# A two-path decoder step on one core: the conv's shifted input copied on chip, the sample issued 15 units later, its decode held back beside attention, and one norm's waits filled

## The chip, the cores and the metric

The program runs on one core of one Trainium2 chip. A core has five engines with queues of their own: TensorE (PE in the profile, PEld for its weight loads), VectorE (DVE), ScalarE (ACT), GpSimd (POOL) and SyncE (SP, which here only issues DMAs). ScalarE and GpSimd issue DMAs too. The metric is the device time of one execution in microseconds; smaller is better.

## What is computed

The reference runs one trunk over two inputs: a prompt (512 tokens, no past) and a sample (8 sequences of 4 new tokens, each with 2048 past keys and values in pages). Width 1024, 16 heads of 64, two layers. Layer 0 is a convolution module and an MLP; then keys and values are projected; layer 1 is attention and an MLP.

```python
def post_norm_residual(x, y, gate, g, b):
    return layer_norm(DEEPNORM_ALPHA * x + (1.0 + gate) * y, g, b)

def conformer_conv(h, conv_prev, ...):
    a, g = jnp.split(h @ pw1_w + pw1_b, 2, axis=-1)
    u = a * jax.nn.sigmoid(g)
    full = jnp.concatenate([conv_prev, u], axis=1)
    y = depthwise_conv(full, dw_w, width=31) + dw_b
    y = jax.nn.silu(layer_norm(y, ln_g, ln_b))
    return y @ pw2_w, full[:, -30:]

def stick_breaking(q, k, v, bias, q_pos, k_pos):
    z = q . k * HEAD_DIM ** -0.5 + bias
    log_rem = where(mask, log_sigmoid(-z), 0)
    after = suffix sum of log_rem over the later keys
    w = where(mask, exp(log_sigmoid(z) + after), 0)
    return w . v
```

Every sub-layer takes h = x * (1 + scale) + shift with scale, shift and gate from a product of silu(c) with ada_w. The MLP is square(relu(h @ w1)) @ w2 with 4096 inner columns. Outputs are y, the new conv state and the new keys and values of both inputs.

## The kernel before

**Layout.** The prompt stands feature by feature: 8 tiles of 128 features x 512 tokens. Its weights come in by ScalarE's DMA queue (stage), are split on ScalarE (whi) and VectorE (wlo) into a high and a low part, and every product is three matmuls (lines 327, 330, 331; tiles pw in the conv's first product, pd elsewhere). The sample has 32 rows only. Its products take the weights as the moving operand straight from a load on SP's queue (sw, tiles w_acc and sd_acc), and its norms are small steps on VectorE with a sum over features by two tiny matmuls (smp).

**Order of the work.** Sample and prompt are two generators, `sample()` and `prompt()`, and a loop at the end of the kernel advances the one whose clock is behind. Each yield adds a cost: DEC_COST 10 for a step of the sample's decode, ML_COST 2.6 for a piece of the prompt's MLP, AT_COST 12 for one of eight head pairs of the prompt's attention. The sample's clock starts at CLK0 = -20, that is 20 units ahead. The order that comes out is static: each engine has one queue, worked in order. A scheduler may still move an instruction by its priority.

**The conv.** The prompt's gated product u of the 8 feature tiles (k) goes two ways. For two of them (TAPS) VectorE does the 31 taps itself (line 690, tile v out of upad). For the other six u is stored to DRAM (ud, line 877, GpSimd's queue) and read back four times, shifted by 0 to 3 columns (ur, line 703, GpSimd's queue, two buffers): 32 channels times 4 shifts fill the 128 partitions, and 64 products of 128 x 32 weights (wk, made on VectorE, line 707) give one cv tile (line 713). Its statistics (lnT transposes on TensorE, bn on VectorE) follow for each tile, then the norm: VectorE makes mean and rstd, a diagonal matrix dg, and a product with ones spreads them over the partitions (mb, rb, line 386); lines 420 and 421 apply them.

**The other norms** of the prompt work alike; make_h (lines 441 to 466) then gives the split operands xhi (ScalarE) and xlo (VectorE) for the next product. ada_B (line 246) are products of the modulation with weights loaded on SP's queue (adaw), issued between.

**The decode.** For each of 8 sequences s there are 4 key steps, a weights step and 4 value steps. A key step gathers kraw by an indirect DMA of GpSimd (index tile krow), transposes it on VectorE in 128 x 512 pieces (kt, line 1065) and multiplies with qb (zt, line 1071). The weights step has two scans (fx, line 1089), the product z_s (line 1103) and transposes wT. A value step gathers vt (index tile vrow) and multiplies (av, line 1122). krow and vrow come from the page table by 16 small operations of VectorE and two more (lines 1036 to 1040).

**The prompt's attention** works head pair by head pair on units of query blocks: logits pz, two sigmoids on ScalarE (afx, as), a scan on VectorE (line 1423), a product (line 1424), transposes awt, products with the values oP, and at the end of a pair xlo (line 1440).

**The end.** The last MLP block runs in two halves of 256 tokens (v, line 1469), with transposes lnT back to token rows (yt), statistics bn, and for each half mean and rstd by small steps (lines 431 to 438). Of the first half two yt tiles go over ScalarE and GpSimd (lines 1482 to 1484, with nmr = -mean x rstd from VectorE), the other six over VectorE (lines 1486 and 1488). The sample's result is yrow (lines 1167 and 1168), stored on SP's queue as the yt tiles are.

## Time and profile before

| | us |
|---|---|
| median of 3 runs | 1649.97 (1649.86 to 1650.26) |
| the profiled execution's own time | 1648.19 |
| its span, first to last instruction | 1646.4 |
| TensorE busy | 1554.2 (94%) |
| VectorE busy | 955.3 (58%) |
| ScalarE busy | 569.1 (35%) |
| GpSimd busy | 171.8 (10%) |
| mean DMA rate | 249 GB/s |

Busy times are sums over the whole span, in which stages with different limits follow one another: conv product (to about 160 us), conv and its norm (to 270), MLP 0 (330 to 797), keys, values and q (to 990), attention (to 1115), output product and norm (to 1225), MLP 1 (to 1632) and the last norm. So they are read again by stretch. A matmul's end is modelled, and a busy TensorE need not run at its peak: the granted clock (1.00 is 2.4 GHz, 0.50 is 1.2 GHz) stands beside each stretch.

### The profile page before, as it was taken

The page shows a single profiled execution, that of the slowest core. Times are in us where ns is not written, and L with a number is a line of the kernel's source. Part 1 is how long each engine was busy: PE and PEld are TensorE (multiplying, and loading weights), DVE is VectorE, ACT ScalarE, POOL GpSimd, SP SyncE. Part 2 cuts the span into 40 slices and gives each one's busy share as a digit, 9 for nine tenths or more (in the row PEclk, how much of TensorE's full clock was granted, in tenths as well). Part 3 has the DMA queues.
Part 4 walks back from the last instruction along what each step waited for, and adds up shares of the span by engine and source line. Part 5 has one row for each costly group of instructions (what it writes and reads, how often), then busy time and mean ns, then how long its engine had stood idle before and what let it go on. Part 6 is the DMA issues. An engine that isn't in the chain of part 4 may idle for free.

```text
span 1646.4 us, 25072 instructions
## 1 busy us (share of the span) xinstructions
PE 1554.2 (94%) x10297; PEld 1078.2 (65%) x10297; DVE 955.3 (58%) x1822; ACT 569.1 (35%) x905; POOL 171.8 (10%) x197
## 2 busy tenths in 40 slices
PE   6999989989999999999899899889899999999996
PEld 4666325656777777777477675557767767656886
DVE  4599536475676655665644448985765434332547
ACT  2322114262332333323332545852362323223332
POOL 1110200000112121110012012021002100000001
PEclk9999999999999999999999999999999999999998
DMA  9898879688667767676888878365546585995221
GB/s 321 267 338 298 241 271 368 240 327 313 230 230 278 281 248 251 215 258 230 323 286 297 330 255 325 109 238 193 202 154 232 181 332 181 353 345 190 83 74 52
DMA packets 148261, 409.23 MB, mean 249 GB/s; under 512 B 8197, under 2 KB 74021, under 8 KB 123555
## 3 DMA queue, kind: packets, MB, share of 16 engines
q1 hardware_dynamic: 48771, 161.86, 26.3%
q0 software_dynamic: 22944, 149.07, 25.2%
q10 hardware_dynamic: 76432, 96.70, 17.6%
q8 instruction: 81, 1.33, 0.3%
q14 instruction: 33, 0.27, 0.0%
HBM read 390.56 MB, written 17.88 MB: 248 GB/s over the span
## 4 chain that ended last, share of the span: by engine, by line
PE 75%; issue 9%; DMA 7%; DVE 6%; ACT 2%; POOL 1%; DVEq 0%; POOLq 0%; ACTq 0%; SPq 0%
PE pd L327 18%; PE pd L331 17%; PE pd L330 17%; PE zt L1071 3%; PE sd_acc L551 3%; PE av L1122 3%; PE cv L713 2%; DMA adaw<-in_ada_w_dram 2%; PE w_acc L578 2%; PE pw L327 1%; PE pw L330 1%; PE pw L331 1%; DMA stage<-in_conv_pw_w_dram 1%; PE ada_A L246 1%; PE lnT L366 1%
## 5 line engine op out<-in xcount | busy, mean ns | idle before, releaser
L319 DVE TENSOR_TENSOR wlo<-stage,whi 128x1024 fp32r<-128x1024 f32 x184 | 223.7, 1218 | 219.9 <-ACT whi L316 219.6
L316 ACT CAST whi<-stage 128x1024 fp32r<-128x1024 f32 x184 | 191.6, 1046 | 415.2 <-PE pd L331 355.4
L327 PE MATMUL pd<-xhi,whi 128*128 128x512 f32 (+1 forms) x832 | 320.5, 387 | 6.0 <-ACT xhi L454 2.7
L331 PE MATMUL pd<-xlo,whi 128*128 128x512 f32 (+1 forms) x832 | 312.7, 385 | 9.2 <-DVE xlo L460 9.0
L330 PE MATMUL pd<-xhi,wlo 128*128 128x512 f32 (+1 forms) x832 | 318.8, 384 | 2.3 <-DVE wlo L319 2.2
L1065 DVE STREAM_TRANSPOSE kt<-kraw 128x512 f32<-128x512 f32 x256 | 164.3, 686 | 124.0 <-DMA kraw<-in_cache_k_dram,krow 77.5
L327 PE MATMUL pd<-h2h,whi 128*128 128x512 f32 (+1 forms) x544 | 206.5, 388 | 1.6 <-DVE v L1240 1.0
L330 PE MATMUL pd<-h2h,wlo 128*128 128x512 f32 (+1 forms) x544 | 205.1, 382 | 0.0
L331 PE MATMUL pd<-h2l,whi 128*128 128x512 f32 (+1 forms) x544 | 205.0, 383 | 0.0
L331 PEld LDWEIGHTS pd<-xlo,whi 128*128 128x128 f32 x832 | 156.5, 192 | 64.7 <-issue 18.0
L327 PEld LDWEIGHTS pd<-xhi,whi 128*128 128x128 f32 x832 | 160.4, 193 | 56.3 <-issue 13.5
L330 PEld LDWEIGHTS pd<-xhi,wlo 128*128 128x128 f32 x832 | 160.6, 193 | 41.7 <-issue 11.0
L1240 DVE SCALAR_TENSOR_TENSOR v<-pd,mod_B,v 128x512 f32<-128x512 f32 x120 | 87.8, 745 | 117.7 <-PE pd L331 117.4
L1043 POOL DMA_INDIRECT kraw<-in_cache_k_dram,krow x64 | 65.4, 1022 | 625.4 <-DVE kt L1065 391.4
L327 PEld LDWEIGHTS pd<-h2h,whi 128*128 128x128 f32 x544 | 101.9, 188 | 34.9 <-issue 10.4
L1215 ACT ACTIVATE relu<-pd 128x512 f32<-128x512 f32 (+1 forms) x68 | 38.9, 572 | 239.1 <-PE pd L331 233.9
L331 PEld LDWEIGHTS pd<-h2l,whi 128*128 128x128 f32 x544 | 101.8, 188 | 28.6 <-issue 9.4
L330 PEld LDWEIGHTS pd<-h2h,wlo 128*128 128x128 f32 x544 | 102.2, 188 | 25.0 <-issue 6.7
L1043 POOL DMA_INDIRECT vt<-in_cache_v_dram,vrow x64 | 67.0, 1047 | 270.1 <-PE av L1122 220.2
L1071 PE MATMUL zt<-kt,qb 128*32 128x128 f32 x2048 | 75.5, 279 | 5.6 <-DVE kt L1065 5.6
L1071 PEld LDWEIGHTS zt<-kt,qb 128*32 128x32 f32 x2048 | 52.7, 110 | 30.9 <-issue 17.5
L368 DVE BATCH_NORM_STATS2 bn<-lnT 128x6 f32<-128x128 f32 x160 | 36.6, 287 | 61.4 <-PE lnT L366 61.1
(300 smaller groups left out, 1928.1 us busy)
## 6 DMA issues: line engine op xcount, KB each, us to landing
sw<-in_mlp_w_dram SPq DMA_DIRECT2D x64, 1024.0 KB
stage<-in_mlp_w_dram ACTq DMA_DIRECT2D x64, 1024.0 KB
adaw<-in_ada_w_dram SPq DMA_DIRECT2D x40, 1024.0 KB
stage<-in_conv_pw_w_dram ACTq DMA_DIRECT2D x10, 1024.0 KB
adaw<-in_ada_w_dram SPq DMA_DIRECT2D x16, 512.0 KB
swkv<-in_w_kv_dram SPq DMA_DIRECT2D x8, 1024.0 KB
stage<-in_w_kv_dram ACTq DMA_DIRECT2D x8, 1024.0 KB
ur<-ud POOLq DMA_DIRECT2D x24, 270.0 KB, 6.6
```

Source lines behind the costliest of these rows:

```text
L316: ins = nc.scalar.copy(hi, st[:, :, c0 : c0 + cw])
L319: ins = vec.tensor_tensor(lo, st[:, :, c0 : c0 + cw], hi.bitcast(F32), op=ALU.subtract)
L327: first = mm(out, whi, xh, start=start, stop=False)
L330: mm(out, wlo, xh, start=False, stop=False)
L331: latest[:] = [mm(out, whi, xl, start=False, stop=stop)]
L551: mm(acc[32 * g : 32 * g + 32, :], hT[:, kk * 2 + kp, :], blk[:, kp * D + c * 512 : kp * D + c * 512 + 512], start=(kk == 0), stop=(kk == ...
L1043: nc.gpsimd.indirect_dma_start(out=out, out_offset=None, in_=cache.rearrange("g (r e) h d -> (g r) (e h d)", e=2), in_offset=bass.Indirect ...
L1065: ins = vec.transpose(kt[:, 2 * x : 2 * x + 2, :], raw[x].rearrange("p (e c) -> p e c", e=2)[:, :, c0 : c0 + 256])
L1071: behind(mm(zt[u][32 * g : 32 * g + 32, f * P : f * P + P], qb[:, u, hh * 8 + bl].rearrange("p x q -> p (x q)"), kt[:, :, bl * 32 : bl * 3 ...
L1122: behind(mm(av[32 * g : 32 * g + 32, :], wT[u][:, i, e, a, :], vt[:, e * D + u * 512 : e * D + u * 512 + 512], start=(a == 0 and i == 0), ...
L1215: latest_act[:] = [act(r, a, AF.Relu)]
L1240: ins = vec.scalar_tensor_tensor(v[kt][:, ts], a, gt[:, kt, 8:9], v[kt][:, ts], op0=ALU.mult, op1=ALU.add)
```

## The change

Seven things are changed. (1) CLK0 goes from -20 to -5. (2) AT_COST goes from 12 to 4. (3) For the six conv tiles ud, its padding and the ur loads are gone: u is written into the tile y, and 16 copies of 32 partitions x about 512 columns, with two memsets, build ur. For the first two tiles all copies are ScalarE's, spread over the first product; for the other four half are VectorE's. (4) krow and vrow are made where the sample's first dense product is issued (the column of row numbers comes with c1), and bias_p and the page table load behind the axd store. (5) The sample's state_out (the urow copies and eight stores) stands ahead of its MLP 0 instead of behind. (6) One norm (after MLP 0) has 4 + 5 + 4 idle products of 128 x 128: behind the last lnT, behind mb, and ahead of the next pd. (7) nmr has the norms' priority.

```diff
-CLK0 = -20.0
+CLK0 = -5.0
...
-AT_COST = 12.0
+AT_COST = 4.0
...
+                idle_products(mb, self.fill[0], self.last)
                 self.spread(mv[:, b0:b1, 0], mb)
+                idle_products(rb, self.fill[1], last_spread[0])
                 self.spread(rstd_of(mv[:, b0:b1, 1], b1 - b0), rb)
+                waiting[:] = [(self.fill[2], last_spread[0])]
                 return mb, rb
+    waiting = []
+
+    def idle_products(out, n, after):
+        for _ in range(n):
+            after = order(mm(out[:, 0:P], onesm, onesm, start=True, stop=True), after)
...
-    def conv_load(k):
+    def conv_load(k, both):
         raw[k] = pld.tile([P, 4, T + 28], F32, tag="ur", bufs=2, name="ur")
-        for j in range(4):
-            pdma(raw[k][32 * j : 32 * j + 32], ud[k].rearrange("(g c) t -> c g t", g=4)[:, :, j : j + T + 28])
+
+        vec.memset(raw[k][:, :, 0 : CW - 1], 0.0)
+        vec.memset(raw[k][:, :, T + CW - 4 :], 0.0)
+        for g in range(4):
+            for j in range(4):
+                out = raw[k][32 * j : 32 * j + 32, g, CW - 1 - j : min(T + CW - 1 - j, T + 28)]
+                src = y[k][32 * g : 32 * g + 32, 0 : out.shape[-1]]
+                if both and (g + j) % 2:
+                    vec.tensor_copy(out, src)
+                else:
+                    order(nc.scalar.copy(out, src), last_whi[0])
+                    yield
...
-                u = tmp("u")
+                u = y[kt]
             vec.scalar_tensor_tensor(u, acc[0], pcol(R_PWB, kt), sg, op0=ALU.add, op1=ALU.mult)
-            if kt not in TAPS:
-                u_dma = pdma(ud[kt][:, CW - 1 : T + CW - 1], u)
...
             if kt in REST[:2]:
-                conv_load(kt)
+                loads.append(conv_load(kt, False))
+            for _ in itertools.islice(itertools.chain(*loads), 5 if kt < KT - 1 else 32):
+                pass
             some_taps(5)
...
         s_ln(n)
+        state_out()
         n = yield from s_mlp(n, 0)
-        state_out()
...
-        nrm = Norm()
+        nrm = Norm(fill=(4, 5, 4))
         yield from p_mlp(*hl, v, 0, nrm, H_0A, H_0B)
...
-                    vec.scalar_tensor_tensor(nmr, mean, -1.0, rstd, op0=ALU.mult, op1=ALU.mult)
+                    with tc.high_priority(LN_PRI):
+                        vec.scalar_tensor_tensor(nmr, mean, -1.0, rstd, op0=ALU.mult, op1=ALU.mult)
```

The static order of the two kernels shows what the two planner numbers move. Line numbers in the changed kernel are larger by 3 to 21 (1065 is 1083, 1423 is 1443, 1424 is 1444, 1440 is 1460, 1469 is 1489, 1486 to 1488 are 1507 to 1509).

VectorE amid the prompt's attention, before (afx, as: one head pair's scans and products; kt: the decode's transposes):

```order
L1065 STREAM_TRANSPOSE kt<-kraw 128x512 x2
L1423 SCALAR_TENSOR_TENSOR afx<-afx 128x384 x2
L1424 TENSOR_TENSOR as<-as,afx 128x383
L1440 TENSOR_TENSOR xlo<-oP,xhi 128x512
L1424 TENSOR_TENSOR as<-as,afx 128x383
L1065 STREAM_TRANSPOSE kt<-kraw 128x512 x2
L1423 SCALAR_TENSOR_TENSOR afx<-afx 128x512 x2
L1065 STREAM_TRANSPOSE kt<-kraw 128x512 x2
L1424 TENSOR_TENSOR as<-as,afx 128x511 x2
L1423 SCALAR_TENSOR_TENSOR afx<-afx 128x128
```

Six kt transposes of the decode stand among ten operations of the attention here. The same head pair's place in the changed kernel:

```order
L1444 TENSOR_TENSOR as<-as,afx 128x127
L1444 TENSOR_TENSOR as<-as,afx 128x255
L1444 TENSOR_TENSOR as<-as,afx 128x127
L1444 TENSOR_TENSOR as<-as,afx 128x255
L1443 SCALAR_TENSOR_TENSOR afx<-afx 128x384 x2
L1444 TENSOR_TENSOR as<-as,afx 128x383
L1460 TENSOR_TENSOR xlo<-oP,xhi 128x512
L1444 TENSOR_TENSOR as<-as,afx 128x383
L1443 SCALAR_TENSOR_TENSOR afx<-afx 128x512 x2
L1444 TENSOR_TENSOR as<-as,afx 128x511 x2
```

The six transposes are gone from this place. Over the whole attention kt falls from 42 to 18; on TensorE the rows of zt there fall from 176 to 96 and those of av from 40 to 16. The removed steps come behind the attention, and the sample's products with wo, which stood at the 3428th of the prompt's 4416 full-width products, now stand at the 3780th; its w1 blocks go from the 3585th to the 3952nd and its w2 blocks from the 3753rd to the 4135th, ending at the 4298th.

VectorE in the norm ahead of MLP 0's first product, before (v, xlo: the prompt's norm and operands; krow, sv, sred: the sample's index arithmetic and norm):

```order
L420 TENSOR_TENSOR v<-v,mrb 128x256
L1040 TENSOR_SCALAR krow<-krow,c_3339 128x64
L1040 TENSOR_SCALAR vrow<-vrow,c_3339 128x64
L539 TENSOR_TENSOR sv<-sv,sax 128x256
L421 TENSOR_TENSOR v<-v,mrb 128x256
L460 TENSOR_TENSOR xlo<-h,xhi 128x256
L420 TENSOR_TENSOR v<-v,mrb 128x256
L513 TENSOR_REDUCE sred<-sv 128x32
L421 TENSOR_TENSOR v<-v,mrb 128x256
L460 TENSOR_TENSOR xlo<-h,xhi 128x256 x3
```

Four of these rows are the sample's. The same steps of the prompt in the changed kernel:

```order
L473 TENSOR_TENSOR xlo<-h,xhi 128x256
L433 TENSOR_TENSOR v<-v,mrb 128x256
L434 TENSOR_TENSOR v<-v,mrb 128x256
L473 TENSOR_TENSOR xlo<-h,xhi 128x256
L433 TENSOR_TENSOR v<-v,mrb 128x256
L434 TENSOR_TENSOR v<-v,mrb 128x256
L473 TENSOR_TENSOR xlo<-h,xhi 128x256
L433 TENSOR_TENSOR v<-v,mrb 128x256
L434 TENSOR_TENSOR v<-v,mrb 128x256
L473 TENSOR_TENSOR xlo<-h,xhi 128x256
```

The sample's index arithmetic and norm are gone from between them; the norm now stands behind, at the prompt's next v (row 459 on), and the index arithmetic near the span's beginning.

VectorE at the end, behind the prompt's last v (bn: statistics, the second half's; yt: the prompt's result), before:

```order
L1469 SCALAR_TENSOR_TENSOR v<-pd,mod_B_6802,v 128x256 x2
L368 BN_STATS bn_13510<-lnT 128x6 x6
L376 BN_AGGR mv<-bn_13510 128x2 x2
L1486 SCALAR_TENSOR_TENSOR yt<-yt,mv,gb 128x512
L431 TENSOR_SCALAR ve<-mv 128x2
L1486 SCALAR_TENSOR_TENSOR yt<-yt,mv,gb 128x512 x3
L432 TENSOR_SCALAR rw<-ve 128x2
L434 TENSOR_SCALAR vh<-ve 128x2
```

The first half's small steps and nmr are through by then. In the changed kernel, with the first half's small steps and nmr among them:

```order
L1489 SCALAR_TENSOR_TENSOR v<-pd,mod_B_6981,v 128x256
L371 BN_STATS bn_13590<-lnT 128x6 x6
L445 TENSOR_SCALAR rw<-ve 128x2
L447 TENSOR_SCALAR vh<-ve 128x2
L371 BN_STATS bn_13590<-lnT 128x6 x2
L446 TENSOR_SCALAR rs<-rw 128x2
L371 BN_STATS bn_13590<-lnT 128x6 x4
L449 TENSOR_TENSOR rw<-rs 128x2
L379 BN_AGGR mv<-bn_13590 128x2 x2
L450 TENSOR_TENSOR rw<-rw,vh 128x2
L1507 SCALAR_TENSOR_TENSOR yt<-yt,mv,gb 128x512
```

The first half's rstd (rw, rs on 128 x 2) is still being made between the second half's statistics. VectorE some twenty rows later:

```order
L451 SCALAR_TENSOR_TENSOR rs<-rw,rs 128x2
L450 TENSOR_TENSOR rw<-rw,vh 128x2
L1498 SCALAR_TENSOR_TENSOR nmr<-mv,rs 128x2
L1509 SCALAR_TENSOR_TENSOR yt<-yt,rs,gb 128x512 x2
L451 SCALAR_TENSOR_TENSOR rs<-rw,rs 128x2
```

Before the change nmr stood ahead of all of these; now it stands behind 12 statistics and four yt steps. On TensorE the sample's yrow products stood at the 4057th of the prompt's 4416 full-width products and now stand at the 4388th, among the last lnT.

## Rows read from the trace of the kernel before

**Rows 1.** The page's busy times: engine, us, share of the span, instructions.

```profile
PE 1554.2 (94%) x10297; PEld 1078.2 (65%) x10297; DVE 955.3 (58%) x1822; ACT 569.1 (35%) x905; POOL 171.8 (10%) x197
```

**Rows 2.** Busy by stretch: length, PE, PEld, DVE, ACT, POOL, clock, DMA share, GB/s.

```profile
200.00:275.00 75.00, 65.18 (x432) 27.13 (x432) 41.19 (x106) 24.27 (x38) 5.45 (x10) 0.91 0.84 303
300.00:350.00 50.00, 43.05 (x291) 29.13 (x289) 34.85 (x136) 17.78 (x35) 0.00 (x0) 0.94 0.61 223
1000.00:1050.00 50.00, 43.71 (x450) 25.66 (x450) 46.79 (x84) 32.34 (x64) 8.76 (x8) 0.93 0.68 258
1050.00:1115.00 65.00, 55.78 (x630) 35.91 (x627) 58.22 (x103) 43.12 (x85) 9.91 (x10) 0.97 0.53 183
1350.00:1510.00 160.00, 159.62 (x811) 99.81 (x811) 54.74 (x77) 43.83 (x61) 0.00 (x0) 1.00 0.77 286
1625.00:1646.00 21.00, 7.02 (x57) 6.38 (x55) 17.15 (x55) 4.40 (x17) 5.50 (x4) 0.71 0.26 100
```

**Rows 3.** TensorE's waits over the span: us in total, times, longest.

```profile
PE pd L331 <- DVE xlo L460: 9.0, 6, 2.9
...
PE zt L1071 <- DVE kt L1065: 5.6, 3, 2.2
```

**Rows 4.** TensorE in order of time, in the conv: start, us.

```profile
208.71 6.14 PE L713 MATMUL cv<-ur,wk 128*32 128x512 f32 x32 [4.30 <-DMA ur<-ud]
```

**Rows 5.** TensorE's groups, 160 to 233 us: busy, mean ns, idle before.

```profile
L713 PE MATMUL cv<-ur,wk 128*32 128x512 f32 x384 | 50.0, 624 | 4.3 <-DMA ur<-ud 4.3
```

**Rows 6.** Three tiles' instructions: duration ns min/median/max, first and last start.

```profile
L946 DVE COPY qr<-qr x3: 684/684/687, 394.0 to 395.4; 32x1024 f32<-32x1024 f32 x3
...
L1261 DVE COPY ucrow<-ucT x2: 668/670/671, 245.5 to 246.1; 30x512 f32<-30x512 f32 x2
...
L556 ACT COPY sd_sb<-sd_acc x5: 562/586/589, 189.9 to 1509.3; 128x512 f32<-128x512 f32 x5
```

**Rows 7.** VectorE's groups, 160 to 233 us.

```profile
L368 DVE BATCH_NORM_STATS2 bn<-lnT 128x6 f32<-128x128 f32 x24 | 5.4, 286 | 20.3 <-PE lnT L366 20.3
L707 DVE TENSOR_TENSOR wk<-c,wtap 128x1024 f32<-128x1024 f32 x4 | 4.9, 1225 | 3.8 <-PE cv L713 3.8
...
L690 DVE SCALAR_TENSOR_TENSOR v<-upad,prm,v 128x512 f32<-128x512 f32 x3 | 2.3, 777 | 0.0
```

**Rows 8.** VectorE's groups, 328 to 348 us.

```profile
L1037 DVE TENSOR_SCALAR vrow<-ptab 32x32 int32<-32x32 int32 x8 | 1.4, 174 | 0.0
```

**Rows 9.** A stretch of the norm after MLP 0, columns as in Rows 2.

```profile
816.00:819.00 3.00, 3.00 (x12) 1.10 (x12) 2.93 (x6) 3.00 (x5) 0.00 (x0) 0.50 1.01 408
```

**Rows 10.** VectorE's groups in the attention, 1000 to 1112 us.

```profile
L1065 DVE STREAM_TRANSPOSE kt<-kraw 128x512 f32<-128x512 f32 x38 | 24.7, 686 | 5.5 <-DMA kraw<-in_cache_k_dram,krow 5.5
...
L1089 DVE TENSOR_TENSOR_SCAN fx<-fx 128x512 f32<-128x512 f32 x2 | 2.4, 1220 | 0.0
```

**Rows 11.** TensorE's groups in the attention, 1000 to 1115 us.

```profile
L1071 PE MATMUL zt<-kt,qb 128*32 128x128 f32 x320 | 15.1, 292 | 5.6 <-DVE kt L1065 5.6
...
L1122 PE MATMUL av<-vt,wT 128*32 128x512 f32 x64 | 9.7, 599 | 1.1 <-DMA vt<-in_cache_v_dram,vrow 1.1
```

**Rows 12.** The sample's last w2 block and its last store, in order of time.

```profile
1508.12 1.06 PE L551 MATMUL sd_acc<-sw,h2T 128*32 128x512 f32 x8
...
1544.33 0.35 SPq L1169 DMA_DIRECT2D out_dram<-yrow  x1
```

**Rows 13.** VectorE and GpSimd at the end, in order of time.

```profile
1629.66 2.44 DVE L1488 SCALAR_TENSOR_TENSOR yt<-yt,rs,gb 128x512 f32<-128x512 f32 x2
1632.02 0.86 DVE L1469 SCALAR_TENSOR_TENSOR v<-pd,mod_B,v 128x256 f32<-128x256 f32 x2
...
1640.35 2.74 DVE L1488 SCALAR_TENSOR_TENSOR yt<-yt,rs,gb 128x512 f32<-128x512 f32 x4
...
1630.17 3.06 POOL L1483 TENSOR_TENSOR yt<-yt,gb 128x512 f32<-128x512 f32 x2 [310.90 <-ACT yt L1482]
1633.18 2.48 POOL L1484 TENSOR_TENSOR yt<-yt,gb 128x512 f32<-128x512 f32 x2
```

More of the change, by code (lines that the diff above doesn't have):

```diff
@@ L67 @@
 NR = 56
[L69 removed]
+C1_W = 128 + 32 + 64 + 32 + 3
 C2_W = 512 + 512 + 128 + 128 + 20
@@ L679, in yoco_step_kernel @@
     raw = {}
+    loads = []
     TAPS = (0, 2)
@@ L717, in conv @@
         if k in REST[:-2]:
-            conv_load(REST[REST.index(k) + 2])
+            for _ in conv_load(REST[REST.index(k) + 2], True):
+                pass
     sy = sfm("sy", "sv", 2)
@@ L1176, in p_tiles @@
         out = [pm("pd")[:, 0 : ts.stop - ts.start] for _ in w]
+        while waiting:
+            idle_products(out[0], *waiting.pop())
         for k in range(nk):
```

42 lines of the change are left out of this document (19 added, 23 removed).

## The prediction

> **What bounds the kernel now.** I read the whole-span busy table first, then busy time by stretch, then who TensorE waited for, then the groups of instructions inside the two stretches the change reorders, and last the end in order of time. TensorE is busy 1554.2 us of the 1646.4 us span [rows 1], so a change that leaves TensorE's work as it is can only win what stands between its work: idle time and time at a lower granted clock. The stretches show where that is [rows 2]. From 1350 to 1510 us, where the sample's MLP runs beside the prompt's, TensorE is busy 159.62 of 160 us: no room. In the attention, 1000 to 1115 us, it is busy 43.71 + 55.78 = 99.5 of 115 us, at 0.93 and 0.97 of full clock, while VectorE is busy 46.79 + 58.22 = 105.0. VectorE sets the pace there. From 300 to 350 us (the norm ahead of MLP 0's first product) 6.95 us are idle and the clock takes some 43.05 x 0.06 = 2.6 us more. From 1625 to the end only 7.02 of 21 us are TensorE's; the rest is VectorE's last norm. The list of waits names the same engine: it stood 9.0 us for xlo and 5.6 for kt, both VectorE's [rows 3].
>
> The profiled execution took 1648.19 us, 1.79 us outside its span, and the median of three runs is 1649.97. I make the sum on the profiled execution and add 1.8 us for the median.
>
> **Conv input copied on chip.** Gone are 24 loads of ur, 6 stores of ud and the padding stores, all on GpSimd's queue, and the one wait that they caused: TensorE stood 4.30 us for ur, and the 32 products behind it took 6.14 us [rows 4], where the other eleven groups of 32 took (50.0 - 6.14) / 11 = 4.0 [rows 5]. So 4.3 + 2.1 = 6.4 us can go. In its place each of six blocks needs 16 copies of 32 x 512, eight of them on VectorE and eight on ScalarE (the first two blocks all on ScalarE). The trace has no such copy. The nearest rows: VectorE copied 32 x 1024 from SBUF to SBUF in 684 ns, half of which with a share of fixed cost is about 0.37 us; from PSUM it copied 30 x 512 in 670 ns; ScalarE took 586 ns for 128 x 512 from PSUM [rows 6]. I take 0.37 on VectorE, the same kind of source and target, and keep 0.67 as the upper end. Per block VectorE then has 8 x 0.37 = 3.0 us of copies, one wk (1.23), eight statistics (8 x 0.23 = 1.8) and 14/6 filter taps of 0.78 (1.8), which the change puts later [rows 7]: 7.8 us, 8.6 with the two memsets and small sample steps. TensorE's 64 products and their transposes take 8.0 + 0.6 us. They are level, so some of the wait comes back: 2 to 4 us in all. ScalarE's eight copies, 8 x 0.59 = 4.7 us, lie inside the block. So the conv itself gives -3. The sample 15 units later leaves the conv's norm fewer filler blocks, and puts sample norm steps and two urow copies ahead of its second spread: +3, since that stretch (200 to 275 us) is already idle 9.8 us [rows 2]. Together 0, from -4 to +6; at 0.67 us a copy 4 x 8 x 0.3 = +10.
>
> The Trainium skill (VectorE: DVE Perf Modes, section "Mode 2×_2P — use both read ports for one tensor") says that a one-source fp32 copy runs at twice the rate only with source and target in SBUF and an outermost dimension that is even, or odd and equal on both sides. The two copy rows agree with the SBUF half of it (684 ns for 1024, 670 ns for 512 from PSUM); that copies of 511 elements keep the rate no run here shows.
>
> **Index arithmetic moved.** krow and vrow leave the norm of MLP 0 and run about 80 us into the span, where VectorE already works hard on the first product's operands. With what goes with it, +1 us (0 to +4).
>
> **MLP 0's first norm.** Sixteen small operations with 1.4 us on vrow alone [rows 8], as much on krow, and the sample's post-norm chain (about 10 us of VectorE in all between 328 and 348 us) no longer stand among the make_h steps that xlo waits for. There are 6.95 + 2.6 = 9.5 us to be had [rows 2]. I take 7, because the prompt's own chain of some 24 half-tile operations stays: -7 (-11 to -2).
>
> **Fills at one norm.** At the norm after MLP 0 the granted clock reads 0.50, the lower of TensorE's two levels, from 816 to 819 us, though TensorE is busy all of it [rows 9]: 3 x 0.5 = 1.5 us lost there, perhaps 3 with its neighbours. Thirteen 128 x 128 products fill idle time and can keep the clock. But ada_B blocks that wait for weights now stand between them ahead of mb and rb, and so do the sample's wT transposes: 0 (-3 to +4).
>
> **Attention.** A unit of prompt attention now counts 4 instead of 12, so eight units advance the clock by 32 instead of 96, and the planner issues less decode work among them. On VectorE 42 kt transposes among the attention become 18; two scans fx, two qb, two z_s, am and the small steps leave too. 24 x 0.686 = 16.5 us, and fx 2.4 [rows 10], and about 4.4 for the rest: 23 us off the engine that sets the pace. TensorE loses zt 176 to 96 rows of the order, 45% of 15.1 us, and av 40 to 16, 60% of 9.7 [rows 11]: 6.8 + 5.8 = 12.6 us. That work isn't gone: it lands in MLP 1, where TensorE has no room, and lengthens it by its full size. Net 23 - 12.6 = about -10 us. If VectorE also keeps the 5.5 us that it stood for kraw [rows 10], -14 at best; if the attention turns TensorE-bound (99.5 - 4.7 for the clock - 12.6 = 82 us of work against VectorE's 82, so they are level) and keeps its present share of idle time, 13%, the stretch shrinks by 20 and the net is -7; -4 is my upper end. What is late next in the attention is TensorE itself.
>
> **The end.** The sample's last store was issued at 1544.33 [rows 12], 100 us ahead of the end; now yrow is issued 28 full-width products (6.5 us) ahead of TensorE's last, and its store directly ahead of the prompt's last stores on SP's queue. On VectorE the sample's last norm (some 25 operations) stands among the prompt's last v, and the first half's statistics come after yrow. nmr, which ran before 1629.66, now comes behind the second half's statistics: after the last v remain 12 statistics instead of 6, four yt steps and some 20 small ones, about 9.3 us, then nmr. From nmr on, ScalarE's yt (0.8) and GpSimd's 3.06 + 2.48 us [rows 13] make 6.9 us with the gaps. Before, from the last v (1632.02 + 0.86) to the last yt's end (1640.35 + 2.74) were 10.2 us; now 9.3 + 6.9 = 16.2: +6. With a little standing of TensorE for smp and yrow +7 (+3 to +11).
>
> VectorE's two yt steps beside GpSimd took 2.44 us, 1.22 each, while four of them later took 2.74, 0.69 each [rows 13]. They slow one another, and my 6.9 us holds that: six at up to 1.22 are 7.3. The Trainium skill (SBUF — State Buffer, section "Who interferes with whom") states it harder: an operation of VectorE with two inputs in SBUF and one of GpSimd that reads SBUF exclude one another; an estimate by that is 6 x 0.69 + 5.54 = 9.7 us in place of 6.9, and the end +10. It speaks against this change; the row of 1.22 us shows a part of it.
>
> **Sum.** Conv 0, index arithmetic +1, MLP 0's norm -7, fills 0, attention -10, the end +7: -9 us. 1648.2 - 9 = 1639 profiled, 1641 us as a median, -0.55%.
>
> **Rivals.** (A) Work is only moved. If TensorE bounds the attention as soon as VectorE is relieved, or MLP 1 gets new waits for the decode's operands, the attention gives 0: 1 - 7 + 7 = +1, so 1650 us (no change). For it speaks that the two engines come out level, and that kt and kraw now arrive in MLP 1; against it that VectorE was busy over 90% of the attention and TensorE 86%. Chance 0.14. (B) The sample becomes the end. Its last chain of product, reduce, mean, reduce, small steps and transposes had 35 us from the end of the last w2 block (1508.12 + 1.06) to its store (1544.33) [rows 12]; now about 90 full-width products of 0.23 us and some small ones lie between, about 23 us. TensorE's queue is in order, so smp or yrow that waits stops the prompt's products behind it. From the point where the chain needs over 23 us each us more is an us of time; at 32 us it is +9 on top of the +7, and with -5 from the attention and -2 from MLP 0's norm instead of my values, 1650 + 1 + 16 - 7 = 1660 us (slower). The chain's own durations add up to about 11 us, which speaks against; its 35 us before speak for. Chance 0.13. (C) VectorE binds the conv: the copies cost 0.67 us, the conv +10: 1651 us, no change. Chance 0.08. (D) Better than forecast: the conv's 6.4 us go entirely, the clock holds at the filled norm, the attention -14: 1641 - 3 - 3 - 4 = 1631. Chance 0.15. The forecast has 0.50.
>
> **Chances and range.** A measurement of this kernel tells about 0.2%, 3.3 us, from no change. The forecast with its own range 1633 to 1646 and (D) are faster, with a little of (A) and (C): 0.68. Within 0.2%: most of (A) and (C), 0.16. Slower: (B) and the tails of (A) and (C), 0.16. The range for 8 in 10 goes from 1626 to 1654.
>
> **What would show it.** Attention: VectorE's busy time near 82 us there and TensorE's idle time below 10; if the stretch is 20 us shorter and MLP 1 12 us longer, the step is right. MLP 0: the wait for xlo around 330 us gone. Conv: copy rows near 0.37 us, no wait for ur over 2 us a block. Filled norm: a granted clock of 1.00 through the stretch and no wait for adaw over 2 us. The end: some 27 us without much of TensorE instead of 21, GpSimd's yt last. The forecast is wrong if smp or yrow shows waits of several us, or if the first stretch after attention has new idle time.

## The result and the profile of the changed kernel

The changed kernel takes 1668.33 us (median of four runs, 1666.27 to 1669.43) against 1650.12 for the kernel before on the same chip: 1.0119 [1.0103, 1.0136], 1.2% slower. The forecast was 1641 and the range ended at 1654. The profiled execution took 1668.12 us, 1.8 outside its span, as before.

The busy page of the changed kernel, engines in the order of [rows 1]:

```profile
span 1666.3 us, 25161 instructions
PE 1559.4 (94%) x10323; PEld 1084.3 (65%) x10323; DVE 973.3 (58%) x1866; ACT 607.8 (36%) x969; POOL 153.0 (9%) x164
```

The span grew by 19.9 us, TensorE's busy time by only 5.2. To see where, I cut both spans at the same counts of the prompt's full-width products and took, of each piece, the idle time of TensorE plus its busy time times (1 - granted clock). I call that the loss of a piece:

| piece (products) | loss before | loss after | forecast of the difference |
|---|---|---|---|
| 0 to 500: first product, conv, its norm | 40.1 | 37.9 | 0, index arithmetic +1 |
| 500 to 700: start of MLP 0 | 10.8 | 6.5 | -7 |
| 2000 to 2300: the filled norm | 9.3 | 9.5 | 0 |
| 2500 to 2630: ahead of the attention | 7.5 | 10.2 | none |
| 2690 to 2850: the attention and part of the output product | 23.1 | 36.6 | -10 |
| 2850 to TensorE's last product | 17.0 | 17.1 | none |
| behind it | 13.1 | 19.2 | +7 |
| all, with small pieces | 121.0 | 137.2 | -9 |

The other 3.7 us of the 19.9 are TensorE's own work at full clock; the fills, whose 26 instructions take some 3 us, count as work here. The windows of the changed kernel that answer to [rows 2] (busy us of each engine, granted clock, DMA share, GB/s); the last is the stretch behind TensorE's last product:

```profile
200.00:275.00 75.00, 67.56 (x422) 33.91 (x415) 52.40 (x138) 30.51 (x48) 3.83 (x7) 0.93 0.59 220
300.00:350.00 50.00, 45.09 (x314) 29.57 (x311) 30.44 (x99) 29.91 (x57) 0.00 (x0) 0.97 0.90 325
1000.00:1050.00 50.00, 39.92 (x387) 24.80 (x388) 38.95 (x66) 25.50 (x50) 6.22 (x6) 0.81 0.56 205
1050.00:1115.00 65.00, 52.52 (x463) 35.31 (x462) 48.22 (x82) 45.98 (x91) 0.00 (x0) 1.00 0.15 41
1646.90:1666.30 19.40, 0.45 (x2) 0.05 (x1) 14.63 (x42) 2.96 (x10) 5.12 (x4) 0.50 0.29 108
```

From 1000 to 1050 us VectorE is busy 38.95 us where it was busy 46.79 [rows 2]: the relief came. TensorE stands 10 us all the same, and its clock is 0.81. The list of what TensorE waited for (us in all, times, longest) has a new first line, a wait inside the prompt's own attention that was 2.3 us before, and a second one for whi (ScalarE's split of the weights), 2.5 us before, of which 6.7 us come in one piece ahead of the attention; xlo and kt are a little smaller than in [rows 3], and ur is gone from it:

```profile
PE oP L1455 <- ACT aw L1449: 20.2, 20, 3.0
PE pd L330 <- ACT whi L318: 9.1, 5, 6.7
...
PE pd L334 <- DVE xlo L473: 7.8, 9, 1.8
PE zt L1089 <- DVE kt L1083: 4.9, 4, 3.1
```

### The profile page after: what moved, and what is told of

It is laid out like the page before. It is cut to its first block, busy times and chain, and to the rows that moved or that the text cites. A ratio compares the mean times of both kernels' runs of the same rounds, so it can differ in the third digit from the quotient of the medians.

```text
span 1666.3 us, 25161 instructions
## 1 busy us (share of the span) xinstructions
PE 1559.4 (94%) x10323; PEld 1084.3 (65%) x10323; DVE 973.3 (58%) x1866; ACT 607.8 (36%) x969; POOL 153.0 (9%) x164
## 3 DMA queue, kind: packets, MB, share of 16 engines
q10 hardware_dynamic: 76432, 96.70, 17.1%
## 4 chain that ended last, share of the span: by engine, by line
PE 73%; issue 10%; DVE 8%; DMA 5%; ACT 3%; POOL 1%; DVEq 0%; POOLq 0%; ACTq 0%
PE pd L330 17%; PE pd L334 16%; PE pd L333 16%; PE zt L1089 3%; PE cv L735 3%; PE av L1140 3%; PE sd_acc L564 2%; PE w_acc L591 2%; DMA kraw<-in_cache_k_dram,krow 1%; DMA adaw<-in_ada_w_dram 1%; DMA stage<-in_conv_pw_w_dram 1%; PE oP L1455 1%; ACT afx L1434 1%; PE pw L333 1%; PE pw L330 1%
## 5 line engine op out<-in xcount | busy, mean ns | idle before, releaser
L330 PEld LDWEIGHTS pd<-h2h,whi 128*128 128x128 f32 x544 | 101.9, 188 | 37.2 <-issue 10.8
L1061 POOL DMA_INDIRECT vt<-in_cache_v_dram,vrow x64 | 68.1, 1065 | 345.4 <-PE av L1140 303.5
L1140 PE MATMUL av<-vt,wT 128*32 128x512 f32 x512 | 65.6, 597 | 0.2 <-DMA vt<-in_cache_v_dram,vrow 0.2
```

Of the source, the lines that this page charges most:

```text
L330: first = mm(out, whi, xh, start=start, stop=False)
L1061: nc.gpsimd.indirect_dma_start(out=out, out_offset=None, in_=cache.rearrange("g (r e) h d -> (g r) (e h d)", e=2), in_offset=bass.Indirect ...
L1140: behind(mm(av[32 * g : 32 * g + 32, :], wT[u][:, i, e, a, :], vt[:, e * D + u * 512 : e * D + u * 512 + 512], start=(a == 0 and i == 0), ...
```

## Experiments on the two planner numbers

First the offset CLK0 and the weight AT_COST are set back in the changed kernel, one by one and both.

```diff
-AT_COST = 4.0
+AT_COST = 12.0
```

> The changed kernel with AT_COST back at 12 (36 kt transposes in the attention instead of 18), all else as changed. Theory R (round trip): the attention is paced by its own chain over four engines (logits, sigmoids on ScalarE, scan and product on VectorE, transposes on TensorE, copy on ScalarE, product with the values), and the decode filled its gaps for nothing. Taking it out cost: TensorE's wait for the copies aw (20.2 us in the changed kernel, 2.3 before) should fall to under 4 us, the attention should lose about 10 us less of TensorE's time than in the changed kernel, the sample should end some 245 full-width products earlier and the last 20 us should fall to about 14: 1645 us. Theory V (VectorE sets the attention's pace, as I forecast; the loss is in conv, fills or the end of the kernel): the attention gets longer by 10 us or more, and the time stays at 1665 or rises.

Measured: 1655.81 us, 1.0037 [1.0019, 1.0055]. With the old weight of attention two thirds of the loss are gone, but not in the way that either theory had it. In the one profile TensorE's wait for aw fell to 1.6 us as theory R said, yet the attention lost 33.3 us, only 3.3 less than in the changed kernel; the end lost 13.1 instead of 19.2.

```diff
-CLK0 = -5.0
+CLK0 = -20.0
```

> The changed kernel with CLK0 back at -20, AT_COST stays at 4: the sample is about 52 full-width products (12 us) earlier at the end, and even less decode stands in the attention (10 kt transposes instead of 18). Theory R: the attention keeps its loss or loses some us more, since still more filling is gone; the end gains back the 6 us that the sample's tail cost there: 1664 us. Theory V: the attention is relieved further, 1655 us or less. If the later sample (CLK0) were the whole harm: 1650.

Measured: 1664.81 us, 1.0103 [1.0066, 1.0140]. Hardly better, though the attention's loss fell from 36.6 to 24.0 and the end's from 19.2 to 13.0: the start of MLP 0 now lost 24.8 us instead of 6.5.

```diff
-CLK0 = -5.0
+CLK0 = -20.0
-AT_COST = 4.0
+AT_COST = 12.0
```

> The changed kernel with both planner numbers back (AT_COST 12, CLK0 -20): what is left is the conv copied on chip, the moved index arithmetic and state_out, the fills and nmr. Theory R: conv and MLP 0's first norm keep the 9 us of TensorE's time that the changed kernel had won by its 400th us, the fills give nothing: 1643 us. Theory V: the parts other than the planner numbers are the harm: over 1655 us.

Measured: 1663.57 us, 1.0090 [1.0058, 1.0123], the same as with the weight 4. With the early sample the weight is worth nothing that can be told; what costs 14 us is the rest of the change.

The weight alone in the kernel before:

```diff
-AT_COST = 12.0
+AT_COST = 4.0
```

> The kernel before with AT_COST 4 alone (10 kt transposes in the attention instead of 38). Theory R: TensorE waits about 20 us for aw, the attention gets hardly shorter while the decode's 15 us of TensorE work come back in MLP 1: 1662 us (1658 to 1668). Theory V, as I forecast for this part: 10 us faster, 1640 us.

Measured: 1647.69 us, 0.9987 [0.9969, 1.0004]: no change that can be told, and neither theory's time. Its windows over the whole attention show why. The first row is of the kernel before, the second of this one:

```profile
993.80:1127.40 133.60, 115.74 (x1229) 72.36 (x1228) 111.69 (x196) 82.41 (x159) 21.02 (x21) 0.96 0.58 211
```

```profile
994.10:1112.30 118.20, 94.78 (x907) 60.80 (x906) 87.01 (x148) 78.27 (x153) 6.53 (x7) 0.99 0.33 114
```

VectorE lost 24.7 us of work, as forecast (23), and the stretch became 15.4 us shorter. But 322 of TensorE's matmuls left with it, and they come back in MLP 1, which has no room for them. TensorE is idle 23.4 us where it was idle 17.9, though VectorE is now busy 74% instead of 84%. Who it waits for:

```profile
PE oP L1435 <- ACT aw L1429: 19.9, 22, 1.0
```

These are 22 short waits in the prompt's own chain (product, sigmoid, scan, product, transpose, copy, product). The held-back kt and av were what TensorE did in those gaps. No engine is full there: from 1030 to 1090 us of this kernel TensorE is busy 77% of the time, VectorE 81% and ScalarE 77%. That the chain sets the pace is read from these waits; no run changed the chain itself.

## Experiments on the start of MLP 0

I first suspected state_out(), whose transfers now stand ahead of the sample's MLP 0 on SP's queue. It goes back behind that MLP, in e3's kernel and in e1's:

```diff
-        state_out()
         n = yield from s_mlp(n, 0)
+        state_out()
```

> As e3 (both planner numbers back), and state_out also back behind the sample's MLP 0. In e3 SP's queue stood 13.6 us for the urow copies, at 216 to 230 us, with the loads for the sample's MLP 0 queued behind, and TensorE later lost 25 us between the 500th and 700th product, where the DMA runs at over 400 GB/s, against 10.8 before. Theory Q (queue): that wait is e3's harm. The loads start 13 us earlier, the loss falls to about 11 and the time to 1650 us or less (about 1647 with the conv's gain). Theory C (the conv's copies, the moved index arithmetic or the fills are the harm): it stays over 1657 us.

> As e1 (AT_COST 12, CLK0 -5), with state_out back behind the sample's MLP 0. Theory Q: with the sample 15 units later its MLP 0 loads are wanted later, and the wait on SP's queue costs less than with CLK0 -20; 1650 to 1655 us against e1's 1655.8. The attention's loss in e1 (33 us, against 24 with CLK0 -20) stays, if it comes from where the later sample's decode meets the attention; it goes, with 10 us, if it came from state_out's place.

Measured: e5 1657.51 us, 1.0052 [1.0029, 1.0074]; e6 1655.91, 1.0043 [1.0026, 1.0060], the same as e1. In e5 the start of MLP 0 still loses 24.8 us, so the store's place isn't the cause of that; its 6 us against e3 stand between intervals that overlap a little, and I leave them open.

Next, the conv's input back through DRAM, in e5's kernel (index arithmetic, fills and nmr stay); then the same with either planner number as the change has it:

```diff
-                u = y[kt]
+                u = tmp("u")
...
+                u_dma = pdma(ud[kt][:, CW - 1 : T + CW - 1], u)
...
+            pdma(raw[k][32 * j : 32 * j + 32], ud[k].rearrange("(g c) t -> c g t", g=4)[:, :, j : j + T + 28])
```

> As e5 (planner numbers and state_out back), and the conv's shifted input through DRAM again as before: what is left of the change is the moved index arithmetic, the fills and nmr's priority. Theory S (the sample's chain in the conv): with copies and late taps VectorE is busy 33.6 of 35 us between 165 and 200 us and works the sample's some 20 dependent norm steps one by one between them; shT comes at 211 us instead of 184, the DMA stands at 33 GB/s meanwhile, and the sample's MLP 0 stalls TensorE from 328 to 355 us. Then this kernel has shT near 184 us, a loss of 7 to 11 us between the 500th and 700th product instead of 25, and 1645 to 1649 us. Theory C2 (moved index arithmetic or the fills are the harm): it stays near e5, 1655 us or more.

```diff
-AT_COST = 12.0
+AT_COST = 4.0
```

> As e10 with AT_COST 4. The decode is held back beside the attention with the sample early, so that no gather is waited for there. By the theory that held-back decode only moves TensorE's work (e4: 1647.7 against 1649.6) this is e10's time within 3 us; by my forecast for this part 10 us faster than e10.

```diff
-CLK0 = -20.0
+CLK0 = -5.0
```

> As e10 with the sample 15 units later (CLK0 -5), AT_COST 12, conv through DRAM. If the later sample is good by itself (the first norm of MLP 0 freed of the sample's steps, as I forecast), the loss between the 500th and 700th product falls to 5 or 6 us, and the time lies below e10's, if the attention does not lose more. If the later sample meets the attention badly whatever the conv does (as in e1 with 33 us lost there), it is 5 to 10 us slower than e10.

Measured: 1654.63 us, 1.0031 [1.0015, 1.0047]; 1654.41, 1.0035 [1.0019, 1.0051]; 1661.12, 1.0072 [1.0047, 1.0097]. The loss at the start of MLP 0 is 9.5, 9.5 and 7.1 us. So the loss at MLP 0 went back as theory S said, but e10's time missed its 1645 to 1649: between 300 and 500 products it loses 22.2 us where the kernel before lost 15.9. The later sample alone costs some 6.5 us (1661.12 against 1654.63) when the conv goes through DRAM; its loss between 150 and 500 products is 35.6 us, against 24.1 in e10. With the copies on chip it gains 8 when state_out stands ahead of the sample's MLP 0 (e1 against e3), and 1.6, which can't be told, when it stands behind as it does here (e6 against e5). So the 15 units hurt with the conv through DRAM and don't with the copies: the copies make the sample late, and the 15 units give it a place in the order to which it can be in time. In the changed kernel the sample is late too, but the start of MLP 0 loses only 6.5 us.

The copies by themselves, in the kernel before, and the index arithmetic by itself:

```diff
-    def conv_load(k):
+    def conv_load(k, both):
...
+                if both and (g + j) % 2:
+                    vec.tensor_copy(out, src)
+                else:
+                    order(nc.scalar.copy(out, src), last_whi[0])
+                    yield
```

> The kernel before with the conv's input copied on chip alone (bias_p and the page table behind the axd store, since the last store of ud that they stood behind is gone; index arithmetic, state_out, fills, nmr and planner numbers as before). Theory S: shT over 205 us, and 20 to 25 us lost between the 500th and 700th product: 1657 us. By my forecast for this part alone: 1649 us, with 6 us of the conv's waits gone.

```diff
-    with tc.issue_after(u_dma.ins):
+    with tc.issue_after(axd_dma.ins):
...
+        krow = base.tile([P, NS, 4, 2], I32, name="krow")
+        vrow = base.tile([P, NS, 4, 2], I32, name="vrow")
...
-        krow = sq.tile([P, NS, 4, 2], I32, name="krow")
-        vrow = sq.tile([P, NS, 4, 2], I32, name="vrow")
```

> The kernel before with the index arithmetic made beside the sample's first dense product and the loads of bias_p and the page table put behind the axd store, nothing else. Theory K: these two loads and some 30 small operations now stand in front of the conv's stores and taps, the conv's input comes later and e10's 6 us excess (22.2 us lost between the 300th and 500th product instead of 15.9) is theirs: 1654 us. Theory F: they are hidden, and e10's excess is the fills' or chance of the schedule: 1648 us.

Measured: the copies alone 1659.5 us, 1.0059 [1.0039, 1.0078], with a loss of 26.8 us at the start of MLP 0; the index arithmetic alone 1653.74, 1.0021 [1.0001, 1.0040], at the edge of what can be told. In the first the conv itself gains (35.0 us lost up to the 500th product, 40.1 before). In the second TensorE waits 7.0 us for ur instead of 4.3, a wait that the changed kernel doesn't have, and its loss between 300 and 500 products is 22.5 us, as in e10.

How the copies delay the sample is seen on VectorE. Windows from 165 to 200 us, first before, then with the copies alone:

```profile
165.00:200.00 35.00, 35.00 (x296) 12.18 (x295) 18.57 (x56) 5.70 (x10) 8.53 (x16) 1.00 0.83 245
```

```profile
165.00:200.00 35.00, 35.00 (x300) 11.28 (x302) 33.62 (x82) 19.58 (x32) 0.00 (x0) 1.00 0.10 31
```

VectorE went from half busy to full (33.62 of 35 us). The DMA engines went from 245 to 31 GB/s: twelve loads of ur (270 KB each) that were issued there before are gone with the conv's way through DRAM, and four weight blocks of the sample's MLP 0 (1024 KB each) are now late. The copies are only about half of what came to VectorE. From 165 to 212 us the filter taps (v out of upad), which before the change stood ahead of that stretch but for one, take more of it than the copies (ur). VectorE's groups there, first before, then with the copies alone:

```profile
L690 DVE SCALAR_TENSOR_TENSOR v<-upad,prm,v 128x512 f32<-128x512 f32 x1 | 0.8, 771 | 0.0
```

```profile
L692 DVE SCALAR_TENSOR_TENSOR v<-upad,prm,v 128x512 f32<-128x512 f32 x20 | 14.9, 747 | 0.2
L712 DVE COPY ur<-v 32x512 f32<-32x512 f32 (+2 forms) x32 | 13.4, 419 | 0.7
```

VectorE's timeline in that stretch (start, us), first before, where the sample's norm steps follow one another every 0.22 us, then with the copies alone, where the same steps (L439, L440, L441) have taps, wk and copies between them and need 6.4 us for three:

```profile
179.16 0.19 DVE L436 TENSOR_TENSOR rw<-rs 128x32 f32<-128x32 f32 x1
179.39 0.19 DVE L437 TENSOR_TENSOR rw<-rw,vh 128x32 f32<-128x32 f32 x1
179.62 0.19 DVE L438 SCALAR_TENSOR_TENSOR rs<-rw,rs 128x32 f32<-128x32 f32 x1
```

```profile
181.45 0.18 DVE L439 TENSOR_TENSOR rw<-rs 128x32 f32<-128x32 f32 x1
...
181.69 0.74 DVE L692 SCALAR_TENSOR_TENSOR v<-upad,prm,v 128x512 f32<-128x512 f32 x1
...
182.35 0.18 DVE L440 TENSOR_TENSOR rw<-rw,vh 128x32 f32<-128x32 f32 x1
182.46 1.22 DVE L719 TENSOR_TENSOR wk<-c,wtap 128x1024 f32<-128x1024 f32 x1
183.69 3.50 DVE L712 COPY ur<-v 32x511 f32<-32x511 f32 x8
187.22 0.75 DVE L692 SCALAR_TENSOR_TENSOR v<-upad,prm,v 128x512 f32<-128x512 f32 x1
187.89 0.18 DVE L441 SCALAR_TENSOR_TENSOR rs<-rw,rs 128x32 f32<-128x32 f32 x1
```

The end of that chain is shT, the operand of the sample's product. Its rows before and after the change (duration ns, first and last start):

```profile
L911 DVE TENSOR_TENSOR shT<-shT,sy x1: 425/425/425, 183.6 to 183.6; 128x256 f32<-128x256 f32 x1
```

```profile
L930 DVE TENSOR_TENSOR shT<-shT,sy x1: 407/407/407, 211.2 to 211.2; 128x256 f32<-128x256 f32 x1
```

It is 27.6 us later (207.4 with the copies alone, 191.7 with the conv through DRAM). Four weight blocks of that product stand loaded and hold the ring; SP's own queue, waiting with the next load until the product (sd_acc) has freed one, shows it before and with the copies alone:

```profile
SPq L576 <- PE sd_acc L551: 30.5, 3, 29.7
```

```profile
SPq L579 <- PE sd_acc L554: 57.7, 4, 56.5
```

So the weights of the sample's MLP 0 set out at 209.6 instead of 187.3 us, and its products reach into the start of the prompt's MLP 0, where TensorE, in order, stops for them. That stretch before, and with the copies alone:

```profile
325.00:355.00 30.00, 23.26 (x151) 15.78 (x150) 28.44 (x111) 18.78 (x39) 0.00 (x0) 0.89 0.70 264
```

```profile
325.00:355.00 30.00, 15.55 (x72) 5.97 (x76) 14.38 (x70) 4.20 (x9) 0.00 (x0) 0.62 0.63 239
```

TensorE is idle 14.5 us of 30 and its clock falls to 0.62. Its waits there are for the weights (sw) and the sample's own norm (smp): 5.0 and 6.1 us by name.

If VectorE's load is the cause, the copies on ScalarE alone should help (in e5's kernel):

```diff
-                if both and (g + j) % 2:
+                if False:
```

> As e5, but all 96 copies of the conv's input are ScalarE's (16 a block at 0.62 us, 9.9 us, over TensorE's 8.6 us a block), none VectorE's. Theory S: VectorE is freed of 13 us between 165 and 212 us, shT comes earlier (200 us or before), and the loss between the 500th and 700th product falls by a part of its excess of 14 us, against some 5 us more in the conv: 1650 to 1655 us. If the copies are harmful wherever they run (ScalarE becomes the conv's bound): 1660 us or more.

Measured: 1656.72 us, 1.0045 [1.0029, 1.0061], against 1657.51 of e5. shT comes at 201.1 instead of 211.8, and the loss at the start of MLP 0 falls from 24.8 to 16.7. That is the direction and about half the size; the time itself can't be told from e5's. VectorE is still busy 27.46 us from 165 to 200 us, because 24 taps (17.9 us) stand there too. No run put the taps back to their place with the copies on chip, so how the delay is shared between copies and taps is not shown.

## Experiments on the attention and on the fills

With the late sample and the small weight the attention loses 36.6 us. The suspect is the key gathers. The key steps bunch at its start, and a gather goes out only when the kt steps before it have freed its slot. Rows of the changed kernel on GpSimd, VectorE and TensorE (start, us, what ended the idle time before):

```profile
1006.25 0.94 POOL L1061 DMA_INDIRECT kraw<-in_cache_k_dram,krow  x1 [9.43 <-DVE kt L1083]
...
1012.30 1.30 DVE L1083 STREAM_TRANSPOSE kt<-kraw 128x512 f32<-128x512 f32 x2 [2.92 <-DMA kraw<-in_cache_k_dram,krow]
...
1015.75 0.66 PE L1089 MATMUL zt<-kt,qb 128*32 128x128 f32 x8 [3.13 <-DVE kt L1083]
```

From issue to landing the key gathers of this stretch take 6.7 us, and 5.3 to 10.4 over the whole kernel. GpSimd waited for VectorE, VectorE then for the gather, TensorE then for VectorE, and the prompt's products stood behind zt. At 1030.56 us kt is late for a gather once more; the prompt's own steps on VectorE stand behind it, and TensorE waits 3.05 us for aw. The test leaves the 64 key gathers out: kt is made from a resident constant tile, so the sample's scores come from other data.

```diff
-            raw = [ring("kraw") for _ in range(2)]
-            for x in range(2):
-                gather(raw[x], cache_k, krow[:, s, f, x : x + 1])
...
-  vec.transpose(kt[:, 2 * x : 2 * x + 2, :], raw[x].rearrange("p (e c) -> p e c", e=2)[:, :, c0 : c0 + 256])
+  vec.transpose(kt[:, 2 * x : 2 * x + 2, :], c2[:, 0:512].rearrange("p (e c) -> p e c", e=2))
```

> The changed kernel without its 64 gathers of keys: the transposes kt read a resident constant tile instead, so the sample's attention weights are computed from other data; all arithmetic stays. Theory G (gather): with a later sample the first head pairs of the attention meet key steps whose gathers were issued only when the step ahead was through; kt waits for kraw, TensorE's in-order queue waits for kt (zt, 3.1 us) and the granted clock falls. Without gathers the attention's loss (36.6 us of idle and clock in the changed kernel) falls to 24 or less and the time to about 1655. Theory L (the chain of the attention itself, or chance of the clock): the loss stays over 32 us.

Measured: 1653.19 us, 1.0026 [1.0014, 1.0038], 15 us less than the changed kernel. The attention, after the change and without the gathers:

```profile
983.60:1122.60 139.00, 111.79 (x1034) 73.28 (x1033) 95.89 (x161) 81.05 (x157) 10.00 (x10) 0.93 0.34 116
```

```profile
981.70:1109.00 127.30, 103.88 (x1034) 68.61 (x1033) 95.14 (x161) 80.73 (x157) 4.29 (x4) 1.00 0.23 77
```

The same 1034 matmuls and 96 us of VectorE take 11.7 us less, and the clock is 1.00. The gathers' latency with its consequence for the clock is the extra loss (36.6 to 24.1): TensorE's idle time in these windows falls by 3.8 us, from 27.2 to 23.4, and the lower clock had cost the rest. TensorE's wait for aw stays, 20.1 us without the gathers, and yet the attention then loses no more than about what it lost before the change (23.1). Leaving them out also frees DMA time and ring slots, which this run can't tell from the latency; the other 3 us of the 15 aren't shared out.

Last the fills, alone in the kernel before and with the weight 4:

```diff
-        nrm = Norm()
+        nrm = Norm(fill=(4, 5, 4))
```

> The kernel before with the 13 fills at the norm after MLP 0 alone. If they do what they are for, the granted clock there stays at 1.00 and that norm's loss (9.3 us of idle and clock between the 2000th and 2300th product) falls to about 6, as in e3, e10, e11 and e14: 1646 to 1647 us. If they cost what they add (13 x 0.275 us) and keep the norm's operands waiting: 1652.

```diff
-AT_COST = 12.0
+AT_COST = 4.0
```

> The kernel before with the fills and AT_COST 4. Each is worth 2 or 3 us at most by e4 (1647.7 against 1649.6) and the norm's loss: 1645 us, the best version that these runs point to. If AT_COST 4 is neutral and the fills cost their length: 1650.

Measured: 1650.98 us, 1.0010 [0.9991, 1.0029], and 1652.12, 1.0019 [1.0000, 1.0038]. The windows at the norm of [rows 9], before and with the fills alone:

```profile
813.00:822.00 9.00, 7.37 (x27) 3.97 (x27) 7.77 (x14) 7.36 (x12) 0.00 (x0) 0.62 1.04 394
```

```profile
813.00:822.00 9.00, 6.75 (x48) 4.18 (x48) 7.24 (x16) 5.74 (x10) 0.00 (x0) 1.00 1.02 410
```

The clock stays up, and the norm's loss falls from 9.3 to 5.8 us. The time doesn't show it, and nor does the length of the piece from 2000 to 2300 products, 114.7 us with the fills and 114.3 without: the loss doesn't count the fills' own time. In the kernels with CLK0 -5 that norm loses 9.5 to 11.2 us in spite of the fills. No kernel here was measurably faster than the one before; the nearest was the weight 4 alone, whose interval reaches across 1.

The medians side by side (the kernel before: 1648 to 1650 on the chips concerned). All have the fills, the index arithmetic and nmr; state_out stands ahead of the sample's MLP 0 in the first column, and behind it in the second and in the third:

| | conv on chip | conv on chip, state_out behind | conv through DRAM |
|---|---|---|---|
| CLK0 -20, weight 12 | 1663.6 | 1657.5 | 1654.6 |
| CLK0 -20, weight 4 | 1664.8 | not run | 1654.4 |
| CLK0 -5, weight 12 | 1655.8 | 1655.9 | 1661.1 |
| CLK0 -5, weight 4 | 1668.3 (the change) | not run | not run |

The second and third column are alike but for the conv; their intervals overlap in the first row, and by a little in the third.

## Why the prediction was wrong, point by point

**Attention: the step that failed** (forecast -10, measured +13.5). "VectorE sets the pace there" was read from its busy share. VectorE was relieved of 15.8 us in the changed kernel (111.69 to 95.89) and of 24.7 in e4, for 23 forecast, and zt and av left 13.6 us of TensorE's work to MLP 1 (27.8 to 14.2), for 12.6. But the stretch did not follow VectorE: in the changed kernel it takes 139.0 us where it took 133.6, and e4's 15.4 us of gain are less than the 21.0 us of TensorE's work that left it, so the total stayed: rival (A), by another mechanism (its own sum, +1 on 1650, makes 1651). In all four pairs with the early sample (before and e4, e3 and e2, e10 and e14, e16 and e19) the weight 4 raised the attention's loss, by 0.4 to 5.0 us (one profile each), where I had it fall by 10. No engine's throughput bounds the attention there; by the waits its own chain does (oP for aw, 2.3 to 19.9 us), and the decode was its filler. A busy share of 90% held both the bound and the filler. The step beyond zero, to +13.5, is the gathers (12.5 by e7) and needs the late sample as well: AT_COST 4 moved the time by no more than 1.9 us either way in the four pairs and 12 us with CLK0 -5 (e1 to the changed kernel), 6.1 of them at the end. My sum took the two numbers apart, and the attention with the new start of the sample was nowhere in it. The 5.5 us that VectorE stood for kraw were the right row to look at, but holding the decode back did not save them: over the whole attention VectorE stood 8.3 us for kraw with 44 transposes before, and 7.0 with 24 after.

**Conv** (forecast 0, or +1 with the index arithmetic; measured together -2.2). The wait for ur went, as the working said. The copies' price, rows of the changed kernel:

```profile
L724 ACT COPY ur<-v x64: 612/617/622, 75.7 to 208.4; 32x512 f32<-32x512 f32 x32, 32x510 f32<-32x510 f32 x16, 32x511 f32<-32x511 f32 x16
L722 DVE COPY ur<-v x32: 414/419/423, 178.4 to 209.6; 32x512 f32<-32x512 f32 x16, 32x511 f32<-32x511 f32 x8, 32x510 f32<-32x510 f32 x8
```

0.42 us on VectorE for 0.37 taken, so rival (C) fell; 0.62 on ScalarE for 0.59. What the step left out is who else uses VectorE there. I weighed its 8.6 us a block against TensorE's 8.6 and found them level, with 14 taps over the six blocks; in the changed kernel 25 taps (18.7 us) stand between 165 and 212 us, beside 13.4 us of copies, and VectorE is busy 33.56 us of the 35 up to 200. That leaves no room for a dependent chain of some twenty small steps, and each of these waits for its turn. As a part, in the kernel before, this costs 10 us (e17), none of it in the conv; in the changed kernel, whose sample is 15 units later, shT is as late and no such loss shows.

**MLP 0's norm** (forecast -7, measured -4.3): right in kind and inside its bounds of -11 to -2. xlo is still waited for, up to 1.8 us at a time. **Fills** (0, measured +0.2 in the loss of their norm and +2.2 in its length, 116.5 us for 114.3) and the **index arithmetic** (+1; +4 alone in e18, by a wait for ur that the change has removed) stayed small.

**The end** (forecast +7, measured +6.1). From the last v to the last yt's end are 16.25 us, forecast 16.2, but the halves are wrong by 2 us each: 7.3 up to nmr's end for 9.3, and 8.9 from there for 6.9. Rows of VectorE and GpSimd:

```profile
1652.60 0.16 DVE L1498 SCALAR_TENSOR_TENSOR nmr<-mv,rs 128x2 f32<-128x2 f32 x1
1652.67 1.41 DVE L1509 SCALAR_TENSOR_TENSOR yt<-yt,rs,gb 128x512 f32<-128x512 f32 x2
1654.00 1.23 DVE L451 SCALAR_TENSOR_TENSOR rs<-rw,rs 128x2 f32<-128x2 f32 x1
1655.26 1.19 DVE L449 TENSOR_TENSOR rw<-rs 128x2 f32<-128x2 f32 x1
1656.49 1.19 DVE L450 TENSOR_TENSOR rw<-rw,vh 128x2 f32<-128x2 f32 x1
1657.71 1.18 DVE L451 SCALAR_TENSOR_TENSOR rs<-rw,rs 128x2 f32<-128x2 f32 x1
1658.93 2.74 DVE L1509 SCALAR_TENSOR_TENSOR yt<-yt,rs,gb 128x512 f32<-128x512 f32 x4
```

```profile
1653.75 2.68 POOL L1504 TENSOR_TENSOR yt<-yt,gb 128x512 f32<-128x512 f32 x2 [238.16 <-ACT yt L1503]
1656.40 2.47 POOL L1505 TENSOR_TENSOR yt<-yt,gb 128x512 f32<-128x512 f32 x2
```

Four steps of two elements a partition take 1.2 us each while GpSimd works, against 0.16 directly before. VectorE's yt, not GpSimd's, came last. The rule of the Trainium skill (SBUF — State Buffer, section "Who interferes with whom") that the prediction weighed, exclusion instead of slowing, fits these rows: each small step lasts about as long as one of GpSimd's four instructions (1.2 to 1.3 us). My weighing by that rule, an estimate of 9.7 us for the second half, came closer than the 6.9 that I took, but priced the exclusion for the large steps only; it strikes the small ones hardest. The loss is there only where the sample ends last, in the changed kernel (19.2) and in e7 (20.0); every other kernel has 13.0 to 13.2.

**Rival (B)** had the right sign and the wrong place. From 1500 us on TensorE waited for neither smp nor yrow. Where the sample's lateness did cost, with CLK0 -20, it was at the other end of the kernel, and the chain there, of some 20 small steps too, was in nobody's sum.

**The chances.** 0.16 for slower came mostly from one mechanism at the end; the interaction of two planner numbers and a shared engine had no case.

Open: how much of the attention's loss with CLK0 -5 and weight 12 (33.3 in e1, 25.7 in e6 and e15, one profile each) is the clock's chance; how the delay of the sample's chain is shared between copies and taps; e5's 6 us. The 2.7 us ahead of the attention (9.8 to 12.6 us are lost there in the kernels with CLK0 -5, 4.5 to 9.7 in the others) have a place: in all five kernels with CLK0 -5 TensorE waits there once, 6.2 to 7.4 us, for whi, and ScalarE's whi stands 5.9 to 7.6 us behind stores of axd on ScalarE's own queue; no kernel with CLK0 -20 has that wait. A row of the changed kernel:

```profile
948.24 1.04 ACT L318 CAST whi<-stage 128x1024 fp32r<-128x1024 f32 x1 [6.22 <-DMA axd<-v]
```

The forecast had no term for it.

## What to carry to other kernels

Before work is filled into an in-order engine that then comes out level with its neighbour, list the dependent chains that share it, and whatever else the filling pushes into the same stretch (here the taps): each of their steps waits its turn, and what that delays (weight slots, another loop) can lie some 150 us further on. A stretch where two engines are 85 to 90% busy may be bound by its own chain, with the rest as filler; taking the filler out then gains no more than the time that the filler's own work took, and that is paid where it goes. A loss that counts fills as work falls by the fills' own time, so a fill is judged by the length of its stretch. Two numbers of a planner that both move the same work are tried apart and together: here the weight moved the time by 1.2 us with one offset and by 12 with the other.

## What the runs showed of the hardware

Copies of 32 x 511 and 32 x 510 fp32 elements took the same 0.42 us on VectorE as 512 (414 to 423 ns over all 32), which was open in the prediction; the Trainium skill (VectorE: DVE Perf Modes, section "Mode 2×_2P — use both read ports for one tensor"), with source and target odd and equal, agrees. Unexpected was that a VectorE step of two elements costs 1.2 us beside GpSimd's element-wise work, as much as a large one, so in these rows a chain of small steps beside GpSimd was dearer than the same four steps before it. And the clock fell with the gathers' waits: 0.81 from 1000 to 1050 us after the change, and 0.62, near the lower level of 1.2 GHz, from 1030 to 1040, around the 3.05 us that TensorE stood there; without the gathers it stayed at 1.00 (2.4 GHz) with TensorE busy no longer (38.48 for 39.92 us):

```profile
1000.00:1050.00 50.00, 38.48 (x422) 24.94 (x422) 45.12 (x78) 34.98 (x69) 0.00 (x0) 1.00 0.26 95
```
